# A diffusion transformer layer on one Trainium2 core: written order in the opening and both FFN1 down-projections, spilled chunks in rows of 4 KB, two conditioning vectors computed later

## The chip, the core and the metric

The kernel runs on one core of a Trainium2 chip. The core has a matrix engine (TensorE, called PE in the profile; its weight loads are PEld), three engines for elementwise work (VectorE or DVE, ScalarE or ACT, GpSimd or POOL), a queue that issues DMAs (SyncE or SP) and 16 DMA engines between on-chip memory (SBUF) and device memory (DRAM). Results of TensorE land in PSUM, eight banks of 2 KB a partition.

The metric is device microseconds for one launch of the whole layer. A launch can be profiled; the profile gives each instruction's start and duration, counted from the start of the span, and the clock that TensorE was granted as a share of full speed.

## The reference

One layer over 512 latent tokens (x) and 256 context tokens (ctx), model width 1024, all in float32:

```
ml, mc = adaln(c), adaln(c_ctx)          # silu(cond) @ w_mod + b_mod, 9 vectors of 1024 each
h  = x   + 0.5*ml[2]*rms(swiglu(rms(x)  *(1+ml[1])+ml[0]))*g      # FFN1, latent
hc = ctx + 0.5*mc[2]*rms(swiglu(rms(ctx)*(1+mc[1])+mc[0]))*g      # FFN1, context, same weights
k_c, v_c = keys, values of rms(hc)*(1+mc[4])+mc[3]
y  = mixer(rms(h)*(1+ml[4])+ml[3], k_c, v_c)   # differential attention and gated convolution, merged
h  = h + ml[5]*rms(y)*g
h  = h + 0.5*ml[8]*rms(swiglu(rms(h)*(1+ml[7])+ml[6]))*g          # FFN2, latent
swiglu(z) = (silu(z @ w_gate) * (z @ w_up)) @ w_down              # inner width 2816
```

The nine vectors are numbered m = 0 to 8 below. The context needs m = 0 to 4 only. The change touches FFN1, the vectors and the first part of the mixer (values and context keys).

## The kernel before

**Numbers.** A float32 operand is split into a high part that TensorE reads at its fast float32 format (`hi`, L62, a cast on ACT) and a low part, the rest (`lo`, L67, a subtraction on DVE, or on POOL for every n-th weight, n being `pool_share`). A product is three matmuls: high by high, high by low, low by high. So each weight of 128 x 1024 costs one DMA, one cast and one subtraction (`unit`, `split`) before TensorE can use it.

**Opening (0 to 88 us).** x and ctx lie side by side in 768 columns per group of 128 channels. ACT squares them and TensorE sums for the norm. The vectors 0 and 1 come in four steps, `mod_mm(i)` (matmuls) and `mod_col(i)` (transposing matmuls, then additions on DVE), each for two of the eight channel groups d. `mod_x(d)` scales and shifts group d and makes its high and low parts. `mod_t(p)` takes groups 2p and 2p+1: POOL makes four sums and differences of their column halves (tiles sqt, two buffers), and ACT and DVE make the high and low parts of these. In between, TensorE does the first two of 22 chunks of the inner width directly, in eight steps over k (`open_steps`, L144). `w_load`, `w_pool`, `w_dve`, `w_hi`, `w_lo` load the gate and up weights of a chunk and make sums, differences and their parts. What comes first on an engine in the opening is chosen by the scheduler, apart from a few `issue_after` marks on TensorE.

**Gate-up loop (88 to 395 us).** Chunks 2 to 21 use seven products of half size instead of eight (tiles A, K, G in PSUM banks pa, pb, pc). The first product of chunk 2 writes a pa buffer that the opening's chunks leave when ACT has taken silu of it (L606). Each finished chunk of 768 columns is spilled: high and low parts (tiles hh, hl) are stored with one DMA each. The loop stands inside `with self.in_order()`, which ties each instruction of PE, DVE, ACT and POOL to the one written before it on the same engine; SP is not tied. Vectors 2 and 3 are computed on the side (`mod_early`): `mod_acc` multiplies and adds rows of w_mod on DVE (L556, tiles macc, one 512 KB load for every two rows); `mod_sum` casts the result, sums over partitions on TensorE (tile pd, L107), copies a row on ACT (L572), writes it to DRAM (row_dram, L574), reads it back as columns (L579) and adds the bias on DVE (L581). These are generators; `take(mods, n)` runs n of their steps at fixed places, 5 a chunk.

**Down-projections (395 to 634 us).** `down` runs the 22 chunks twice, first for the 512 latent columns (eight PSUM banks b0 to b7), then for the 256 context columns. For each chunk it loads the spilled parts and one 128 x 1024 weight (f1d), splits the weight, and does 24 matmuls (L731). Beside the latent one, `mod_late` accumulates vectors 4 to 8, five steps a chunk. Beside the context one run the latent result's norm, gate, residual and next modulation (`sandwich`, the tiles yl, sqacc, sqt; taken as `chain`), and the `mod_sum` of vectors 4 to 8, three steps a chunk. Order is chosen by the scheduler here.

**Values and context keys (634 to 734 us).** `values(q, ts)` and `kv_ctx_k(j)` project both streams, while the context's `sandwich` runs as `chain`. Attention, merge and FFN2 follow.

Of the kernel before, what the change touches and what calls it, by code (L numbers as in the profile page):

```python
# [16 lines left out]
P = 128  # L17
# [22 lines left out]
class Builder:  # L40
# [137 lines left out]
    def build(self):  # L178
# [56 lines left out]
        hf_dram = self.t(dp, [NF, 2, P, NKEY], "hf_dram", F32R)  # L235
# [37 lines left out]
        t12, t34 = {}, {}  # L273
# [73 lines left out]
        lat3 = lambda t: t.rearrange("p (s n) -> p s n", s=3)[:, 0:3:2, :]  # L347

        def mod_x(d):

            x = xt[d]
            xl = lat3(x)
            nc.vector.scalar_tensor_tensor(out=xl, in0=xl, scalar=s1[:, 0, d:d + 1], in1=lat3(pbs),
                                           op0=ALU.mult, op1=ALU.mult)
            nc.scalar.activation(xl, xl, AF.Identity, bias=mst[:, 0, 0, d:d + 1], scale=1.0)
            xc = x[:, NCX:2 * NCX]
            nc.gpsimd.tensor_tensor(out=xc, in0=xc, in1=pbs[:, NCX:2 * NCX], op=ALU.mult)
# [6 lines left out]
            else:  # L364
                xeb[d] = self.t(hp, [P, 2, HK], ("hh", "hl")[d // 2 % 2], F32R, bufs=2)
# [5 lines left out]
        def mod_t(p):  # L371
# [9 lines left out]
            tt(out=v[:, 1, :], in0=x2[:, a], in1=u[:, 1, :], op=ALU.subtract)  # L381
            t12[p] = [slot(2 * p + hl, [P, 2, HK], F32R) for hl in range(2)]
# [106 lines left out]
        with tc.issue_after(spread):  # L489
            rows = {0: mod_mm(0)}  # L490
        with tc.issue_after(last["pe"]):
            mod_col(0, rows.pop(0))
        gu0 = [self.split(raw, DM, ring()) for raw in raws[:2]]
        with tc.issue_after(last["pe"]):
            rows[1] = mod_mm(1)
        mod_x(0)
        mod_x(1)
        gu1 = [self.split(raw, DM, ring()) for raw in raws[2:]]
        first = open_steps([gu0, gu1])
        next(first)  # L500
        for i in range(4):
            with tc.issue_after(last["pe"]):
                last["pe"] = next(first)
            if i < 3:
                with tc.issue_after(last["pe"]):
                    mod_col(i + 1, rows.pop(i + 1))
                mod_x(2 * i + 2)
                mod_x(2 * i + 3)
            mod_t(i)
            with tc.issue_after(last["pe"]):  # L510
                last["pe"] = next(first)
            if i < 2:
                with tc.issue_after(last["pe"]):
                    rows[i + 2] = mod_mm(i + 2)
            if i == 2:
                w_load(2)
                w_pool(2)
                w_dve(2)
                w_hi(2, 0)
                w_lo(2, 0)  # L520
                w_hi(2, 2)
                w_lo(2, 2)
# [841 lines left out]
```

## Time and profile before

| | us |
|---|---|
| median of 3 runs (lowest, highest) | 1685.35 (1683.03, 1690.57) |
| the profiled execution | 1684.36 |
| its span | 1682.5 |
| opening | 0 to 88.0 |
| gate-up loop | 88.0 to 395.0 |
| latent down-projection | 395.0 to 534.2 |
| context down-projection | 534.2 to 633.9 |
| values and context keys | 633.9 to 733.6 |
| the rest | 733.6 to 1682.5 |

The mean granted clock of TensorE is 0.984. The times of the stages are starts of the stage's first matmul or the end of the last one before it, from the span's start.

In the lists below a row reads: start, duration, engine, line and operation, output tile from input tiles, shape, count, and in square brackets the idle time before it with what ended it. In a row of waits: who waited for whom, us in total, times, longest. In a row of a group: line, engine, operation, count, then busy us, mean ns of one, and idle time before them.

### The profile page before, as it was taken

To read this page: it belongs to the slowest core of one execution; us is meant where nothing else is said; L and a number is where in the kernel's file an instruction comes from. 1 tells how busy PE (TensorE), PEld (TensorE's weight loads), DVE (VectorE), ACT (ScalarE), POOL (GpSimd) and SP (SyncE) were. 2 spreads that over 40 slices of the span, in tenths; PEclk is the share of its full clock that TensorE was granted. 3 is DMA by queue.
4 is the path that set the end of the run, shared out by engine and by line. 5 is a ranking of instruction groups with operands and counts; after the bars stand their busy time and mean duration, and the time that the engine had idled before them with its cause. 6 is when DMAs were issued, how large, how long until landed. Compare 5 with 4: busy or idle time off the path is not lost. (4 is left out here: it accounts for less than half of the span.)

```text
span 1682.5 us, 23537 instructions
## 1 busy us (share of the span) xinstructions
PE 1598.6 (95%) x8962; PEld 1418.3 (84%) x8962; DVE 1066.9 (63%) x1464; ACT 724.6 (43%) x1137; POOL 268.3 (16%) x205
## 2 busy tenths in 40 slices
PE   5999999998988899999999999999999999999996
PEld 4899999997866789988888888788889998888886
DVE  5687979785657757358877777473347843343345
ACT  4554444442113554335655556442237732222234
POOL 3434434430001232110000000000002100000003
PEclk9999999999999899999999999999999999999998
DMA  9144444447898775687565453632245743232321
GB/s 373 42 154 148 157 144 145 150 144 240 294 311 279 231 238 185 196 256 215 152 171 150 138 150 98 245 134 94 95 150 190 260 132 120 81 107 91 98 76 50
DMA packets 135769, 281.16 MB, mean 167 GB/s; under 512 B 23253, under 2 KB 67925, under 8 KB 135657
## 3 DMA queue, kind: packets, MB, share of 16 engines
q1 hardware_dynamic: 135656, 279.66, 51.7%
q8 instruction: 70, 1.15, 0.3%
q14 instruction: 43, 0.34, 0.1%
HBM read 228.72 MB, written 38.31 MB: 159 GB/s over the span
## 5 line engine op out<-in xcount | busy, mean ns | idle before, releaser
L62 ACT CAST whi<-wraw 128x1024 fp32r<-128x1024 f32 (+1 forms) x262 | 269.4, 1030 | 505.5 <-PE pa L107 95.2
L67 DVE TENSOR_TENSOR wlo<-wraw,whi 128x1024 fp32r<-128x1024 f32 (+1 forms) x250 | 329.4, 1319 | 201.9 <-ACT whi L62 194.5
L107 PE MATMUL f<-xs,whi 128*128 128x512 f32 x640 | 201.6, 394 | 0.0
L107 PE MATMUL pa<-xs,whi 128*128 128x512 f32 (+1 forms) x704 | 195.8, 362 | 0.7 <-ACT ob L968 0.5
L107 PEld LDWEIGHTS pa<-xs,whi 128*128 128x128 f32 x704 | 126.1, 189 | 21.0 <-ACT ob L968 0.7
L107 PEld LDWEIGHTS f<-xs,whi 128*128 128x128 f32 x640 | 118.3, 188 | 23.0
L731 PE MATMUL b<-hh,whi 128*128 128x512 f32 (+1 forms) x352 | 119.9, 352 | 11.5 <-ACT whi L62 7.9
L107 PE MATMUL pa<-xs,wlo 128*128 128x512 f32 (+1 forms) x352 | 127.1, 361 | 1.5 <-DVE wlo L67 1.5
L107 PE MATMUL f<-xs,wlo 128*128 128x512 f32 x320 | 125.1, 391 | 0.0
L731 PE MATMUL b<-hh,wlo 128*128 128x512 f32 (+1 forms) x352 | 112.2, 348 | 11.7 <-DVE wlo L67 6.8
L731 PE MATMUL b<-hl,whi 128*128 128x512 f32 (+1 forms) x352 | 118.4, 343 | 0.6 <-DMA hl<-hf_dram 0.6
L107 PE MATMUL pb<-xs,whi 128*128 128x512 f32 (+1 forms) x448 | 114.4, 344 | 0.0
L160 POOL TENSOR_TENSOR sqacc<-sqacc,sqt 128x256 f32<-128x256 f32 (+1 forms) x20 | 20.0, 1000 | 497.6 <-ACT sqt L158 496.2
L731 PEld LDWEIGHTS b<-hh,whi 128*128 128x128 f32 x352 | 69.7, 199 | 23.9 <-ACT whi L62 13.0
L107 PEld LDWEIGHTS pb<-xs,whi 128*128 128x128 f32 x448 | 78.1, 190 | 9.9
L731 PEld LDWEIGHTS b<-hh,wlo 128*128 128x128 f32 x352 | 65.4, 198 | 22.7 <-DVE wlo L67 10.4
L556 DVE SCALAR_TENSOR_TENSOR macc<-mraw,sc,macc 128x512 f32<-128x512 f32 x84 | 79.8, 1002 | 1.6 <-DMA mraw<-wmodr 1.6
L107 PE MATMUL pb<-xs,wlo 128*128 128x512 f32 (+1 forms) x224 | 77.2, 345 | 0.0
L107 PEld LDWEIGHTS pa<-xs,wlo 128*128 128x128 f32 x352 | 66.5, 189 | 11.7 <-DVE wlo L67 1.7
L731 PEld LDWEIGHTS b<-hl,whi 128*128 128x128 f32 x352 | 69.1, 196 | 8.2 <-DMA hl<-hf_dram 1.3
L936 ACT ACTIVATE e<-s,mx 128x768 f32<-128x768 f32 x64 | 57.1, 898 | 35.1 <-DVE mx L932 35.0
L107 PEld LDWEIGHTS f<-xs,wlo 128*128 128x128 f32 x320 | 60.1, 188 | 12.6
(371 smaller groups left out, 3685.2 us busy)
## 6 DMA issues: line engine op xcount, KB each, us to landing
mraw<-wmodr SPq DMA_DIRECT2D x56, 512.0 KB
wraw<-f2gu SPq DMA_DIRECT2D x56, 512.0 KB
wraw<-f1gu SPq DMA_DIRECT2D x44, 512.0 KB
wraw<-f1d SPq DMA_DIRECT2D x44, 512.0 KB
wraw<-f2d SPq DMA_DIRECT2D x24, 384.0 KB
hf_dram<-hh SPq DMA_DIRECT2D x22, 384.0 KB
hf_dram<-hl SPq DMA_DIRECT2D x22, 384.0 KB
wm<-wmod SPq DMA_DIRECT2D x16, 512.0 KB
```

The lines of the kernel that those rows point to most:

```text
L62: self.nc.scalar.copy(out=out, in_=src)
L67: (eng or self.nc.vector).tensor_tensor(out=out, in0=src, in1=hi.bitcast(F32), op=ALU.subtract)
L107: self.nc.tensor.matmul(out, lhsT=lhsT, rhs=rhs, start=start, stop=stop)
L160: eng.tensor_tensor(out=a, in0=a, in1=s, op=ALU.add)
L556: nc.vector.scalar_tensor_tensor(out=acc, in0=raw[:, k], scalar=s, in1=acc, op0=ALU.mult, op1=ALU.add)
L731: nc.tensor.matmul(o, lhsT=w[:, c], rhs=h[hl], start=start and f + j == 0, stop=f == NF - 1 and j == 2, skip_group_check=True)
L936: nc.scalar.activation(e[m], ps[:, m * NKEY:(m + 1) * NKEY], AF.Exp, scale=SCALE, bias=mx[:, 2 + m:3 + m], accum_out=mx[:, 4 + m:5 + m])
```

## The change

- The opening, and all from the first chunk of the latent down-projection to the end of the context one's chain, also stand under `in_order` (the latter by an ExitStack, closed after `drain(chain)`). The marks of `issue_after` there go.
- In the opening the 768 columns are laid out as half the context, the latent, half the context, and `mod_x` follows. `mod_t(p)` keeps POOL's sums; their parts are made by the new `mod_tp(p)`, one step later. `w_dve(2)` comes after two of the parts.
- A spilled chunk's parts are one tile h. The latent columns go to hl_dram, in rows of 512 x 2 x 4 bytes = 4 KB a partition, and the context's to hc_dram, rows of 2 KB: three DMAs for two. A load of the down-projection is one DMA instead of two.
- `down` loads and splits two chunks ahead (`fetch(f + 2)`). Its first spilled operand is loaded before the last chunk is spilled.
- `mod_sum` takes `wait` steps between its casts and its matmuls (4 in the loop, 3 in the context down-projection, 2 later) instead of one. `mod_late` beside the latent down-projection has vectors 4, 5 and 8, four steps a chunk; vectors 6 and 7 are accumulated and summed beside the values and keys. `pool_share` in the context one is 3 instead of 4.

```
-        hf_dram = self.t(dp, [NF, 2, P, NKEY], "hf_dram", F32R)
+        hl_dram = self.t(dp, [NF, P, 2, NT], "hl_dram", F32R)
+        hc_dram = self.t(dp, [NF, P, 2, NCX], "hc_dram", F32R)
...
+            tsum[p] = u, v
+
+        def mod_tp(p):
+            u, v = tsum.pop(p)
             t12[p] = [slot(2 * p + hl, [P, 2, HK], F32R) for hl in range(2)]
...
+        with self.in_order():
             rows = {0: mod_mm(0)}
...
+            for i in range(4):
+                next(first)
+                if i < 3:
                     mod_col(i + 1, rows.pop(i + 1))
+                    mod_x(2 * i + 2)
+                    mod_x(2 * i + 3)
+                if i:
+                    mod_tp(i - 1)
+                mod_t(i)
+                next(first)
...
+            mod_tp(3)
...
+            h = self.t(hp, [P, 2, NKEY], "h", F32R, bufs=2)
+            self.hi(h[:, 0], g)
+            self.lo(h[:, 1], g, h[:, 0])
+            self.move(hl_dram[f], h[:, :, P:P + NT])
+            for e in range(2):
+                self.move(hc_dram[f][:, :, e * P:e * P + P], h[:, :, e * 640:e * 640 + P])
...
-            yield
+            for _ in range(wait):
+                yield
...
+            h0 = self.t(hp, [P, 2, NT], "h", F32R, bufs=2)
+            self.move(h0, hl_dram[0])
             tail[2]()
             drain(mods)
...
+            fetch(0)
+            fetch(1)
             for f in range(NF):
+                if f + 2 < NF:
+                    fetch(f + 2)
...
-            take(mods, 5)
+        mods = mod_late(((4, (0, 1), 4), (5, (0,), None), (8, (0,), None)))
+        inorder.enter_context(self.in_order())
+        for _ in down(hl_dram, NT, [(p, True) for p in pl], {0: h0}, 0):
+            take(mods, 4)
...
+        for f, _ in enumerate(down(hc_dram, NCX, [(p, d % 2 == 0) for d, p in enumerate(pcs)], {}, 3)):
+            if f:
+                take(chain, 1)
             for _ in range(3):
                 next(next(sums, iter(())), None)
...
+        inorder.close()
...
+        mods = late_sums()
+        values(3, [0, 1, 2, 3, 4, 5])
+        take(mods, 12)
```

First place: POOL in the second half of the opening, before (xs are groups of x, sqt the sums of `mod_t`, s and wraw the weights of chunks 2 and 3).

```order
L357 TENSOR_TENSOR xs_50_145<-xs_50_145,pbs_248 128x256
...
L381 TENSOR_TENSOR sqt_531<-xs_46_137,sqt_530 128x384
L439 TENSOR_TENSOR s_142_715<-wraw_713 128x512
L440 TENSOR_TENSOR wraw_713<-wraw_711,wraw_713 128x512
L439 TENSOR_TENSOR s_172_872<-wraw_870 128x512
L440 TENSOR_TENSOR wraw_870<-wraw_868,wraw_870 128x512
L378 TENSOR_TENSOR sqt_661<-xs_47_139 128x384
...
L381 TENSOR_TENSOR sqt_662<-xs_48_141,sqt_661 128x384
L378 TENSOR_TENSOR sqt_765<-xs_49_143 128x384
```

The same place in the change:

```order
L384 TENSOR_TENSOR sqt_531<-xs_47_138,xs_46_136 128x384
L358 TENSOR_TENSOR xs_50_144<-xs_50_144,pbs_249 128x2x128
L358 TENSOR_TENSOR xs_51_146<-xs_51_146,pbs_249 128x2x128
L381 TENSOR_TENSOR sqt_660<-xs_48_140 128x384
...
L384 TENSOR_TENSOR sqt_661<-xs_49_142,sqt_660 128x384
L446 TENSOR_TENSOR s_137_706<-wraw_704 128x512
L447 TENSOR_TENSOR wraw_704<-wraw_702,wraw_704 128x512
L446 TENSOR_TENSOR s_169_871<-wraw_869 128x512
L447 TENSOR_TENSOR wraw_869<-wraw_867,wraw_869 128x512
L381 TENSOR_TENSOR sqt_764<-xs_50_144 128x384
```

The weight sums of chunks 2 and 3 stood ahead of mod_t(2) and mod_t(3); now mod_t(2) stands ahead of both, behind the last two groups of x, and mod_t(3) behind both.

Second place: DVE from the last chunk's spill (the low part from u) to the first accumulation of `mod_late`, before.

```order
L684 TENSOR_TENSOR u_3627<-n_623_3554,pb_3538 128x384
L581 TENSOR_TENSOR mcx_86<-mcx_86,vec_66 128x8
L67 TENSOR_TENSOR hl_3676<-u_3627,hh_3675 128x768
L553 TENSOR_SCALAR macc_3760<-mraw_3762,sc_80 128x512
L553 TENSOR_SCALAR macc_3761<-mraw_3762,sc_80 128x512
```

The same place in the change:

```order
L67 TENSOR_TENSOR h_3644<-u_3595,h_3644 128x768
L560 SCALAR_TENSOR_TENSOR macc_3524<-mraw_3650,sc_80,macc_3524 128x512
...
L560 SCALAR_TENSOR_TENSOR macc_3525<-mraw_3656,sc_80,macc_3525 128x512
L67 TENSOR_TENSOR mraw_3662<-macc_3524,mraw_3662 128x512
L586 TENSOR_TENSOR ml_85<-ml_85,vec_66 128x8
L67 TENSOR_TENSOR mraw_3672<-macc_3525,mraw_3672 128x512
L586 TENSOR_TENSOR mcx_86<-mcx_86,vec_66 128x8
L557 TENSOR_SCALAR macc_3773<-mraw_3775,sc_80 128x512
```

Eight accumulations of vector 3 (two shown), its two low parts and the two bias additions (L586, which read what came back from DRAM) moved behind the last spill. On PE the two sums of these parts, tiles pd, stand between the last product of the loop and the first matmul of the down-projection.

Third place: DVE in the context down-projection of the change (yl and sqacc are the latent chain; wlo the weights' low parts).

```order
L1265 TENSOR_TENSOR yl_623_3704<-yl_623_3704,res_4675 128x512
L586 TENSOR_TENSOR mcx_86<-mcx_86,vec_66 128x8
L225 SCALAR_TENSOR_TENSOR smc_88<-mcx_86,vec_66 128x8
L67 TENSOR_TENSOR mraw_5027<-xc_701_4081,mraw_5027 128x512
L1262 SCALAR_TENSOR_TENSOR yl_624_3705<-yl_624_3705,gp_14_90,b_812_4761 128x512
L160 TENSOR_TENSOR sqacc_0_817_4774<-sqacc_0_817_4774,sqt_5064 128x512
L67 TENSOR_TENSOR wlo_5078<-wraw_5075,whi_5077 128x1024
```

These rows run in this order now; the bias addition stands ahead of the low part of the weight. Before, nothing fixed them to the order of the program's text.

More of the change, by code (lines that the diff above doesn't have):

```diff
@@ L272, in build @@
         xeb = {}
-        t12, t34 = {}, {}
+        t12, t34, tsum = {}, {}, {}
         def load_mod(d):
@@ L729, in down @@
                     o, start = outs[d]
-                    for j, (w, hl) in enumerate(((wh, 0), (wh, 1), (wl, 0))):
-                        nc.tensor.matmul(o, lhsT=w[:, c], rhs=h[hl], start=start and f + j == 0,
+                    for j, (wt, hl) in enumerate(((wh, 0), (wh, 1), (wl, 0))):
+                        nc.tensor.matmul(o, lhsT=wt[:, c], rhs=x[:, hl], start=start and f + j == 0,
                                          stop=f == NF - 1 and j == 2, skip_group_check=True)
```

127 lines of the change are left out of this document (54 added, 73 removed).

## The prediction

> **What bounds the kernel now.** I read the windows by stage first, then the idle time of TensorE in each stage, then the list of each other engine around those places. The columns are the stretch, its length, then for PE, PEld, DVE, ACT and POOL the busy time with the count, then granted clock, DMA share and GB/s.
>
> ```profile
> PE 1598.6 (95%) x8962; PEld 1418.3 (84%) x8962; DVE 1066.9 (63%) x1464; ACT 724.6 (43%) x1137; POOL 268.3 (16%) x205
> ...
> 21.10:88.00 66.90, 58.22 (x449) 51.99 (x449) 43.55 (x63) 34.16 (x52) 33.35 (x28) 0.90 0.40 152
> 88.00:395.00 307.00, 300.73 (x1697) 295.15 (x1696) 257.54 (x280) 141.06 (x220) 114.77 (x75) 0.99 0.44 151
> 395.00:534.20 139.20, 126.09 (x528) 98.49 (x528) 87.91 (x118) 24.30 (x28) 0.99 (x1) 0.99 0.90 302
> 534.20:633.90 99.70, 83.89 (x585) 78.13 (x586) 70.78 (x91) 52.18 (x78) 33.19 (x17) 0.91 0.74 231
> 633.90:733.60 99.70, 96.20 (x786) 95.52 (x785) 50.57 (x82) 41.44 (x69) 20.73 (x14) 0.98 0.63 203
> ...
> 420.00:440.00 20.00, 20.00 (x90) 16.57 (x89) 16.41 (x23) 3.16 (x3) 0.00 (x0) 1.00 0.88 304
> 500.00:520.00 20.00, 18.24 (x78) 13.99 (x76) 12.17 (x15) 3.19 (x4) 0.00 (x0) 1.00 0.92 322
> ```
>
> TensorE bounds nearly all of it (95%), so a gain can only come out of its gaps. The five stages are the opening, the gate-up loop, the latent and the context down-projection, and the values with the context keys; from 733.6 on nothing is touched. The stretch 420 to 440 shows TensorE never idle: 20.00/90 = 0.222 us a matmul of 512 columns, so 24 of them, one chunk, take 5.33 us, and 22 chunks 117.3. The latent stage has 139.2, some 22 above that. A context matmul has half the columns, so by the same rate 22 chunks take 58.7 and the stage, with 57 other matmuls, has at least 30 us in which TensorE is not at its pace. So both down-projections have something to win; what the written order gives back of it is the question.
>
> **Opening: +11 us, from -6 to +13.** TensorE loses its time here to two short stalls and the half clock behind them.
>
> ```profile
> 63.47 0.44 PE L144 MATMUL pa<-xe,whi 128*128 128x384 f32 x1 [3.20 <-ACT xe L62]
> ...
> 64.60:71.30 6.70, 5.96 (x24) 5.96 (x25) 4.20 (x4) 2.16 (x3) 3.23 (x3) 0.50 0.01 4
> ```
>
> The stall before step k=4 costs 3.2, and the 6.7 us at a granted clock of 0.50 behind it cost half of that, 3.4. In the new order the third column of modulation vectors stands on DVE ahead of the sums' low parts, so I let this stall go: TensorE would end the eight steps some 6 earlier than 88.0. That is the lower end, -6.
>
> But POOL's order changes too (the first excerpt). mod_t(2) now waits for the low parts of mod_tp(1), since the two sum buffers are shared, and these stand on DVE behind x6 and x7.
>
> ```profile
> 58.43 1.28 POOL L439 TENSOR_TENSOR s<-wraw 128x512 f32<-128x512 f32 x1 [4.97 <-DVE wlx L67]
> 62.43 0.99 POOL L378 TENSOR_TENSOR sqt<-xs 128x384 f32<-128x384 f32 x1 [1.38 <-ACT xs L355]
> 75.83 1.02 POOL L378 TENSOR_TENSOR sqt<-xs 128x384 f32<-128x384 f32 x1 [8.01 <-ACT xs L355]
> 79.48 1.72 POOL L381 TENSOR_TENSOR sqt<-xs,sqt 128x384 f32<-128x384 f32 x1
> ...
> 56.04 0.69 DVE L446 TENSOR_TENSOR s<-wraw,s 128x512 f32<-128x512 f32 x1
> 56.04 1.05 ACT L62 CAST whx<-s 128x1024 fp32r<-128x1024 f32 x1 [3.96 <-DVE s L445]
> 57.12 1.23 DVE L67 TENSOR_TENSOR wlx<-s,whx 128x1024 fp32r<-128x1024 f32 x1 [0.39 <-ACT whx L62]
> 81.23 0.84 ACT L62 CAST wm<-sqt 128x768 fp32r<-128x768 f32 x1 [0.84 <-POOL sqt L381]
> 82.09 1.28 ACT L606 ACT_TABLE_LOAD   x1
> 84.37 0.60 ACT L606 ACTIVATE g<-pa 128x512 f32<-128x512 f32 x1 [1.00 <-PE pa L144]
> ```
>
> One mod_t takes 75.83 to 81.20, 5.4. Before, mod_t(2) ran at 62.43 and only mod_t(3) waited, to 75.83, for x6. Now mod_t(2) itself stands behind x6 and x7, and I give it that start, 75.8: its vectors come about 6 earlier, and the low parts of x6, x7 and mod_tp(1) that are put in front of it on DVE take about that. Then, each behind the other: mod_t(2) to 81.2; the weight sum of chunk 2, 1.28, to 82.5; DVE's difference, 0.69, to 83.2; ACT's high part, 1.05, to 84.2; DVE's low part, 1.23, to 85.5. POOL's two sums for chunk 3 wait for this low part, as the row at 58.43 shows (s<-wraw, released by DVE wlx): 2.6, to 88.1. Behind them comes mod_t(3), 5.4, to 93.5, then ACT's last high part 0.84, the table load 1.28 and the first silu 0.6, which stand behind it on ACT: 96.2. That silu frees the PSUM buffer pa that the first product of chunk 2 writes. So TensorE stands from 82 to 96.2, where in the profiled run it went on at 88.0: +8.2. If the half clock behind so long a gap is that behind the gap of 3.2, it adds up to 3.4: +11, with 2.8 of these. The upper end adds 2 for a mod_t(2) that starts so much later.
>
> **Gate-up loop: -5 us, from -7 to -3.** Each modulation sum now waits 4 steps between its casts and its matmuls on TensorE, where it waited one:
>
> ```profile
> PE pd L107 <- ACT mraw L62: 2.8, 3, 1.1
> PE pd L107 <- DVE mraw L67: 2.5, 6, 0.5
> ```
>
> Both waits, 5.3 together, are for those casts, and with three steps more between they go, but for those at the end of the loop. The third DMA of each chunk's spill is hidden by the stage's DMA share of 0.44; SP, which issues it, is named in neither wait.
>
> **Boundary and latent down-projection: +3 us, from -7 to +8.** The early sums took 100 steps, 20 chunks of 5. With three more steps for each of 8 sums they take 124, so 24 are left to the end of the loop, and the order puts them ahead of the down-projection (the second excerpt).
>
> ```profile
> 394.61 0.34 PE L624 MATMUL pa<-xo,wlx 128*128 128x384 f32 x1
> 397.99 0.95 DVE L67 TENSOR_TENSOR hl<-u,hh 128x768 fp32r<-128x768 f32 x1
> 398.55 0.85 PE L731 MATMUL b<-hh,whi 128*128 128x512 f32 x2 [3.60 <-DMA hh<-hf_dram]
> ...
> L556 DVE SCALAR_TENSOR_TENSOR macc<-mraw,sc,macc 128x512 f32<-128x512 f32 x28 | 19.1, 744 | 1.6 <-DMA mraw<-wmodr 1.6
> 385.38 0.69 DVE L67 TENSOR_TENSOR mraw<-macc,mraw 128x512 fp32r<-128x512 f32 x1
> 377.81 0.38 SPq L579 DMA_DIRECT2D ml<-row_dram  x1
> 380.07 0.17 DVE L581 TENSOR_TENSOR ml<-ml,vec 128x8 f32<-128x8 f32 x1 [0.83 <-DMA ml<-row_dram]
> 390.54 0.24 SPq L574 DMA_DIRECT2D row_dram<-macc  x1
> 393.41 0.39 SPq L579 DMA_DIRECT2D mcx<-row_dram  x1
> 397.90 0.17 DVE L581 TENSOR_TENSOR mcx<-mcx,vec 128x8 f32<-128x8 f32 x1 [4.45 <-DMA mcx<-row_dram]
> ```
>
> The spill's low part can end at 398.4 (in the profiled run DVE stood before it, at the addition that waited for a read-back). Then 8 accumulations of 0.744, to 404.3; the low part of the first sum, 0.69, to 405.0; two matmuls, ACT's copy, together some 1.2, to 406.2; the row written and the write landed, 390.54 to 393.41, 2.9; the read-back, 2.3 (377.81 to 380.07) to 4.5 (393.41 to 397.90): 411.4 to 413.6. DVE waits for it before the second sum's low part (0.7), and TensorE does that sum's matmuls (0.6) before the down-projection. It starts near 413, where it started at 398.55.
>
> Behind it, the accumulations took 5 steps a chunk and take 4, and two of the five vectors leave. So the heaviest chunks of the old stage loaded 2.5 blocks of 512 KB of modulation weights beside the chunk's own weights and its spilled operand, 2.36 MB; now chunks 0 to 7 load 1.57 MB, 8 to 15 2.10 MB and the rest 1.05 MB. At 322/0.92 = 350 GB/s (500 to 520, where TensorE is idle for 1.8 of 20 us) 2.10 MB take 6.0 us against 5.33: 5.3 us over eight chunks, of which the prefetch of two chunks and the light chunks ahead hide some. I take 3.5. Then 413 + 117.3 + 3.4 (half clock behind the gap) + 3.5 = 537.2, against 534.2: +3. The ends: no slip and a start at 406.2, with the read-back hidden, -7; a start at 414.6 and all of 7 lost, +8.
>
> The opening's loads have pieces of 3 to 4 KB, and their rate stands in the window
>
> ```profile
> 20.00:40.00 20.00, 15.30 (x117) 11.56 (x117) 12.31 (x16) 10.51 (x16) 12.82 (x12) 0.83 1.02 406
> ```
>
> at 406/1.02 = 398 GB/s a full share. By it the eight chunks take 5.27 us each and the slip is nothing. The rule of the Trainium skill ("DMA: Bandwidth & Descriptors", section "Specifications") is that a transfer of 512 bytes already moves at line rate; by it the 4 KB rows in place of 1 KB rows win nothing and the slip is the 5.3 above. The trace, 398 against 350, speaks against it by 14%, though other queues differ too in these windows. By the one the sum would be 3.5 lower, by the other 2 higher.
>
> **Context down-projection: +3 us, from -15 to +10.** What ACT, DVE and POOL do in this stage, by form, with the idle time ahead of them:
>
> ```profile
> L67 POOL TENSOR_TENSOR wlo<-wraw,whi 128x1024 fp32r<-128x1024 f32 x12 | 30.6, 2549 | 96.0 <-ACT whi L62 95.9
> L67 DVE TENSOR_TENSOR wlo<-wraw,whi 128x1024 fp32r<-128x1024 f32 x18 | 23.9, 1329 | 14.6 <-ACT whi L62 14.6
> L1239 DVE SCALAR_TENSOR_TENSOR yl<-yl,gp,b 128x512 f32<-128x512 f32 x8 | 5.6, 740 | 1.2 <-PE b L107 1.2
> L1242 POOL TENSOR_TENSOR yl<-yl,res 128x512 f32<-128x512 f32 x4 | 5.5, 1384 | 18.4 <-DVE yl L1239 18.4
> L62 ACT CAST whi<-wraw 128x1024 fp32r<-128x1024 f32 x27 | 28.0, 1043 | 18.5 <-DMA wraw<-f1d 11.5 <-PE b L731 6.5 <-DMA wraw<-wv 0.4
> L158 ACT ACTIVATE sqt<-yl 128x512 f32<-128x512 f32 x12 | 7.4, 631 | 5.1 <-DVE yl L1242 1.8 <-POOL sqacc L160 1.3 <-POOL yl L1242 1.0
> ```
>
> ACT now does its evictions and squares of the latent result, ten and more of 0.5 to 0.63, before the first weight's high part, and a low part of 2.55 on POOL comes behind: with some weights made ahead, TensorE starts about 6 late. In the 8 chunks that carry the chain of the latent norm one step hangs on the other through the queues: high part 1.04, low part 1.33, gate 0.74, residual sum 1.38 on POOL (0.7 on DVE), square 0.63; 4.4 to 5.1, partly beside the next, against 2.67 of TensorE. I take 4.5, so 8 x 1.8 = 14. And DVE's additions of a read-back row (the third excerpt) stand in order before low parts of weights, while SP issues the read only behind a write: one stall of about 9 (2.9 for the write, 4.5 for the read, and a low part of 2.55 that SP waits for, less a step) and four of 1.5 to 4.5 (write and read less the three steps between), 20 in all. 58.7 + 6 + 14 + 20 and 4 of half clock are 103, against 99.7: +3. With 5 of the 20 it is -12, with a start 3 earlier -15; with 4.5 for each read +10. I take the middle, since DVE's list shows the additions ahead of the weights that they hold up.
>
> **Values and keys: +2 us, from -2 to +6.** Sixteen loads of 512 KB, 32 accumulations of 0.744 and four sums move in. DVE has 50.57 + 24 of 99.7, the DMA share goes from 0.63 by 8.4 MB at about 340 GB/s a quarter up, under 0.9. So these are hidden by TensorE's products, 96.20 of the 99.7; four sums on TensorE, about 0.6 each, are the 2. Cover gone costs a read-back, 4.5; a granted clock of 1.00 instead of 0.98 would win 2.
>
> The sum is 11 - 5 + 3 + 3 + 2 = +14 on the profiled execution's 1684.4 (span 1682.5 and 1.9 around it), which lies 1.0 below the median of 1685.35: 1698.4, I say 1698.
>
> **The rivals.** *A, faster, chance 0.17:* the context down-projection runs at TensorE's pace. For it: 11.5 of ACT's 18.5 us of idle time there waits for the loads of weights, which the prefetch of two chunks takes away, and two chunks' parts made ahead may lie beside the present chunk's products. Against it: DVE's order, which couples them. With 58.7 + 6 + 10 of read-backs and clock the stage takes 75, and 1698 - 28 = 1670. It decides where the parts of a chunk, overlapped with the next, take under 2.67 us.
> *B, about the same, 0.22:* POOL's chain in the opening is short, because mod_t(2) starts 6 earlier with its vectors. The first product then comes at 90, with some half clock +3 instead of +11, and the latent stage slips by nothing: 1698 - 8 - 3 = 1687.
> *C, slower still, 0.07:* the read-backs take 4.5 us each in every place: +10 for the context stage and +5 more at the boundary and in the latent stage, 1698 + 7 + 5 = 1710.
>
> **How the numbers follow.** My forecast, 0.54, has its own range of 1690 to 1708. The range of 8 in 10 reaches down towards A, 1675, and up to C, 1711. About 0.5%, 8.4 us, is what a measurement of this kernel can tell from no change, so the same is 1677 to 1694. Faster is A and a little of B's lower edge, 0.18; the rest of B and the lower edge of the forecast are the same, 0.27; what is left, 0.55, is slower.
>
> **What would show it.** In the changed profile: no wait for xe before k=4; mod_t(3) on POOL behind the weight sums, and a gap on TensorE of over 10 us before the first 384-column product, with granted clock 0.50 behind it; no waits of pd for mraw in the loop; eight accumulations and a read-back between 398 and 413; 24 matmuls at 5.3 to 5.5 us from there; in the context stage, DVE standing at L586 with <-DMA ml<-row_dram. The prediction is wrong if the first product starts before 90, if the first chunk of the latent stage starts before 406, or if the context stage takes under 85 us.

## The result, and the profile after

The changed kernel takes 1710.49 us (median of 4 runs, 1709.31 to 1712.62), the kernel before 1685.39 beside it: a ratio of 1.0146, 95% interval 1.0120 to 1.0172. It is slower by about 25 us. The time lies in the range that was given, near its upper end, and 12 us above the forecast of 1698.

The windows by stage, first of the kernel before, cut where one stage's last matmul ends, then of the changed one (the columns as in the prediction):

```profile
88.00:394.90 306.90, 300.68 (x1697) 295.15 (x1696) 257.54 (x280) 141.04 (x219) 114.77 (x75) 0.99 0.44 151
533.90:634.00 100.10, 84.03 (x587) 78.23 (x587) 71.18 (x91) 52.58 (x79) 33.19 (x17) 0.91 0.74 231
634.00:768.30 134.30, 130.58 (x939) 123.55 (x938) 73.12 (x117) 53.34 (x86) 25.89 (x18) 0.99 0.70 212
```

```profile
97.80:397.00 299.20, 298.00 (x1692) 294.97 (x1692) 245.82 (x269) 141.01 (x217) 111.91 (x75) 0.99 0.47 154
397.00:413.40 16.40, 2.86 (x4) 1.37 (x5) 8.95 (x14) 3.04 (x5) 1.51 (x2) 0.66 0.38 113
534.40:648.60 114.20, 82.05 (x579) 77.92 (x579) 58.12 (x71) 45.43 (x63) 34.49 (x18) 0.84 0.60 188
648.60:793.10 144.50, 133.94 (x947) 124.80 (x946) 106.88 (x165) 62.96 (x104) 31.87 (x21) 0.99 0.83 250
```

The last row of each reaches to attention's first transposing matmul (t<-ident,a). Set against the prediction's terms, in us:

| stage | before | after | predicted | measured |
|---|---|---|---|---|
| opening, to the first product of chunk 2 | 88.0 | 97.8 | +11 | +9.8 |
| gate-up loop | 306.9 | 299.2 | -5 | -7.7 |
| boundary and latent down-projection | 139.0 | 137.4 | +3 | -1.6 |
| context down-projection | 100.1 | 114.2 | +3 | +14.1 |
| values, keys, to attention | 134.3 | 144.5 | +2 | +10.2 |
| the rest of the span | 914.2 | 914.1 | 0 | -0.1 |
| sum | 1682.5 | 1707.2 | +14 | +24.7 |

What TensorE waited for in the changed kernel, stage by stage (us in total, times, longest):

```profile
PE pa L629 <- ACT g L611: 15.9, 1, 15.9
PE pa L629 <- ACT n L672: 0.6, 2, 0.3
PE pa L629 <- ACT n L651: 0.5, 1, 0.5
...
PE pd L107 <- ACT mraw L62: 10.5, 2, 9.3
PE b L744 <- ACT whi L62: 7.9, 1, 7.9
PE pd L107 <- DVE mraw L67: 3.1, 1, 3.1
...
PE b L107 <- ACT mraw L62: 12.8, 3, 10.8
PE b L107 <- DVE mraw L67: 4.9, 4, 3.7
PE b L107 <- DVE rstd_d L138: 4.4, 2, 4.3
```

The first row is the gap at the opening's end, the next two are all that is left in the loop (the waits of 2.8 and 2.5 for mraw are gone). The three rows after them lie at the two ends of the latent stage, the last three in the context stage. In between TensorE is full: from 420 to 520 it is never idle.

(In the first row of the excerpt of POOL's order in the change, the inputs of the sum at L384 are xs_47_138 and sqt_530; nothing rests on it.)

### The profile page after: what moved, and what is told of

It reads as the page before. It is cut to its first block, busy times and chain, and to the rows that moved or that the text cites. A ratio compares the mean times of both kernels' runs of the same rounds, so it can differ in the third digit from the quotient of the medians.

```text
span 1707.2 us, 23531 instructions
## 1 busy us (share of the span) xinstructions
PE 1593.7 (93%) x8962; PEld 1420.3 (83%) x8962; DVE 1057.7 (62%) x1463; ACT 727.9 (43%) x1139; POOL 272.6 (16%) x208
## 5 line engine op out<-in xcount | busy, mean ns | idle before, releaser
L744 PE MATMUL b<-h,whi 128*128 128x512 f32 (+1 forms) x704 | 178.5, 345 | 7.9 <-ACT whi L62 7.9
L744 PEld LDWEIGHTS b<-h,whi 128*128 128x128 f32 x704 | 127.0, 199 | 23.0 <-ACT whi L62 8.3
L744 PE MATMUL b<-h,wlo 128*128 128x512 f32 (+1 forms) x352 | 121.2, 344 | 2.1 <-POOL wlo L67 2.1
L560 DVE SCALAR_TENSOR_TENSOR macc<-mraw,sc,macc 128x512 f32<-128x512 f32 x112 | 101.0, 940 | 3.7 <-DMA mraw<-wmodr 3.3
L744 PEld LDWEIGHTS b<-h,wlo 128*128 128x128 f32 x352 | 69.5, 198 | 9.5 <-POOL wlo L67 2.6
L872 POOL TENSOR_TENSOR rot<-rot,cossin 128x512 f32<-128x512 f32 x16 | 22.6, 1411 | 252.7 <-DVE rot L871 231.5
L1166 DVE TENSOR_TENSOR silu<-silu,pb 128x512 f32<-128x512 f32 (+1 forms) x28 | 16.0, 573 | 67.0 <-PE pb L107 66.5
```

The source lines that it names most:

```text
L560: nc.vector.scalar_tensor_tensor(out=acc, in0=raw[:, k], scalar=s, in1=acc, op0=ALU.mult, op1=ALU.add)
L744: nc.tensor.matmul(o, lhsT=wt[:, c], rhs=x[:, hl], start=start and f + j == 0, stop=f == NF - 1 and j == 2, skip_group_check=True)
L872: nc.gpsimd.tensor_tensor(out=rt, in0=rt, in1=cs[:, 1, :], op=ALU.mult)
L1166: nc.vector.tensor_tensor(out=a[:, :n], in0=a[:, :n], in1=pu[:, :n], op=ALU.mult)
```

## The experiments

Each is the changed kernel with one edit, until the last four, which join edits. Each ratio is to the kernel before on the same chip. That kernel's median was 1685.0, 1686.9 and 1682.4 in the three groups, so gains are compared by ratios: 0.1% is 1.7 us.

**1. The opening: parts of the sums made earlier.**

```
                 next(first)
+                if i:
+                    mod_tp(i - 1)
                 if i < 3:
                     mod_col(i + 1, rows.pop(i + 1))
                     mod_x(2 * i + 2)
                     mod_x(2 * i + 3)
-                if i:
-                    mod_tp(i - 1)
                 mod_t(i)
```

> The changed kernel, but the parts of the sums (mod_tp(i - 1)) are made before the next column and the next two groups of x, not behind them. Theory: the opening's loss comes from POOL, which waits for the two shared sum buffers; freed earlier, mod_t(2) starts near 61 us and not at 76.9, the weight sums of chunk 3 near 83 and not 87, the first product of chunk 2 near 91 and not 97.8, so the whole takes 6 to 9 us less than the changed kernel's 1710.5: about 1703. Rival: mod_t(3) stands behind the weight sums of chunk 3 on POOL, and these wait for DVE's low part whatever mod_t(2) does; then the first product stays within 2 us of 97.8 and the time within 2 us of 1710.5.

Measured: 1704.95, ratio 1.0120 (1.0095 to 1.0144). POOL's list, of the changed kernel and then of this one:

```profile
76.85 1.66 POOL L381 TENSOR_TENSOR sqt<-xs 128x384 f32<-128x384 f32 x1 [6.97 <-DVE xs L67]
...
87.22 1.91 POOL L446 TENSOR_TENSOR s<-wraw 128x512 f32<-128x512 f32 x1 [1.76 <-DVE wlx L67]
91.03 0.99 POOL L381 TENSOR_TENSOR sqt<-xs 128x384 f32<-128x384 f32 x1
```

```profile
67.28 1.66 POOL L381 TENSOR_TENSOR sqt<-xs 128x384 f32<-128x384 f32 x1 [7.40 <-DVE xs L67]
...
83.63 1.92 POOL L446 TENSOR_TENSOR s<-wraw 128x512 f32<-128x512 f32 x1 [8.42 <-DVE wlx L67]
87.45 0.99 POOL L381 TENSOR_TENSOR sqt<-xs 128x384 f32<-128x384 f32 x1
```

mod_t(2) starts 9.6 earlier, but POOL then stands 8.4 for wlx, and mod_t(3) comes 3.6 earlier only; so does the first product, 94.2. Theory and rival each hold a part: the shared buffers cost something, the weight sums ahead of mod_t(3) more.

**2. All of the early sums in the loop.**

```
-                take(mods, 2)
+                take(mods, 3)
...
-                take(mods, 3)
+                take(mods, 4)
```

> The changed kernel with 7 steps of the early sums a chunk of the gate-up loop (3 and 4) instead of 5 (2 and 3), so that the 124 steps end inside the loop. Theory: the 24 steps left over are what TensorE waits for between the loop and the latent down-projection (16.5 us, 397.0 to 413.4); without them the down-projection starts some 6 us behind the last product, and the time falls by 10 to 12 us, with the half clock behind the gap: about 1699. Rival: DVE is busy for 246 of 299 us in the loop, and the steps push its products' parts back, so the loop grows by as much (8 accumulations of 0.74 us and two sums, 6 to 8 us) and the time falls by less than 4 us.

Measured: 1712.93, ratio 1.0167 (1.0142 to 1.0192): no gain. The gap of 16.4 before the down-projection is gone, but for a wait of 5.6 for a spilled operand, and the loop takes 311 us in place of 299. The rival had the sign. In the loop TensorE now waits 9.2 for the copy n of L672, where it waited 0.6:

```profile
PE pa L629 <- ACT n L672: 9.2, 7, 3.8
```

The longest of these waits, in the lists of ACT and PE:

```profile
140.59 0.62 ACT L62 CAST mraw<-macc 128x512 fp32r<-128x512 f32 x1 [2.73 <-DVE macc L560]
141.11 1.04 ACT L62 CAST whx<-s 128x1024 fp32r<-128x1024 f32 x1
142.06 0.47 ACT L672 COPY n<-pa 128x384 f32<-128x384 f32 x1
```

```profile
142.58 0.62 PE L629 MATMUL pa<-xs,whi 128*128 128x384 f32 x2 [3.81 <-ACT n L672]
```

ACT's cast of a finished sum waits for DVE's last accumulation, and behind it in the written order stands the copy that frees pa. At this place it is not DVE's sum of work but where in the chunk a sum ends; the other six waits, 5.4 together, were not followed.

**3. More steps between a read-back and its use.**

```
             yield
+            if wait == 3:
+                yield
+                yield
+                yield
...
-                     for x in [mod_sum(fp, psf, "b4", 1, m, q, v, 3)] * 7])
+                     for x in [mod_sum(fp, psf, "b4", 1, m, q, v, 3)] * (6 + 4 * q)])
```

> The changed kernel, but in the context down-projection three more steps (one chunk) lie between the read-back of a row and DVE's addition of the bias. Theory: DVE stands at the addition (7.8 us at 577.6 to 585.4) with the low parts of weights behind it in the order, and TensorE with it (10.8, 3.7 and 4.3 us before the sums); with a chunk between, these waits fall to under 2 us each, the stage shrinks from 114 us by 10 to 18 and the time is about 1697. Rival: the stage is set by ACT's and DVE's work of the latent chain in a fixed order, and the wait only shows there; then it shrinks by less than 4 us.

Measured: 1700.4, ratio 1.0098 (1.0070 to 1.0125). The wait in question, in the changed kernel's lists of DVE and of SP:

```profile
585.42 0.17 DVE L586 TENSOR_TENSOR ml<-ml,vec 128x8 f32<-128x8 f32 x1 [7.79 <-DMA ml<-row_dram]
```

```profile
577.48 0.24 SPq L579 DMA_DIRECT2D row_dram<-macc  x1
...
581.18 0.39 SPq L584 DMA_DIRECT2D ml<-row_dram  x1
```

The read is issued 3.7 after the write, and the addition runs 4.2 later; DVE stands until then, with the latent chain and the low parts behind it. With a chunk between, the context stage takes 101.4 us and not 114.2, and TensorE's longest wait for a sum's parts there is 4.9, not 10.8. The 7.9 at the stage's start stays:

```profile
PE b L107 <- ACT mraw L62: 9.7, 3, 4.9
PE b L748 <- ACT whi L62: 7.9, 1, 7.9
```

The theory holds for 13 us of the stage, though not to "under 2 us each"; 2 of them are lost again in the values (146.7 against 144.5).

**4. Pieces of 1 KB again.**

```
-            self.move(hl_dram[f], h[:, :, P:P + NT])
             for e in range(2):
+                self.move(hl_dram[f, e], h[:, :, P + e * 256:P + e * 256 + 256])
...
-                    self.move(h[f], src[f])
+                    if n == NCX:
+                        self.move(h[f], src[f])
+                    else:
+                        for e in range(2):
+                            self.move(h[f][:, :, e * 256:e * 256 + 256], src[f, e])
```

> The changed kernel with the latent columns of the spill in two pieces of 256 columns, so that loads and stores move pieces of 1 KB, as before the change (two loads a chunk instead of one). Theory: the rows of 4 KB are why TensorE lost nothing in the latent down-projection (384 GB/s at a DMA share of 1.00 from 500 to 520 us); with 1 KB the share there reaches 1 at about 345 GB/s, 2.1 MB a chunk take 6.1 us against 5.4, and the stage grows by 3 to 6 us: about 1715. Rival, by the rule of the Trainium skill (DMA: Bandwidth & Descriptors, Specifications) that 512 bytes already move at line rate: nothing changes, and the stage's gain is all from fewer loads a chunk and the prefetch; the time stays within 1.5 us of 1710.5.

Measured: 1709.66, ratio 1.0150 (1.0126 to 1.0173): no change. The heaviest window of the latent stage, with 4 KB and then with 1 KB:

```profile
500.00:520.00 20.00, 20.00 (x90) 16.53 (x90) 9.36 (x10) 4.21 (x4) 0.00 (x0) 1.00 1.00 384
```

```profile
500.00:520.00 20.00, 20.00 (x90) 16.56 (x89) 8.64 (x9) 4.21 (x4) 0.00 (x0) 1.00 0.99 353
```

TensorE is full in both. A full share carries 384 GB/s in the first and 353/0.99 = 357 in the second. But run 1, with rows of 4 KB too, has 345/0.97 = 356 in this window:

```profile
500.00:520.00 20.00, 20.00 (x90) 16.57 (x89) 6.28 (x7) 4.21 (x4) 0.00 (x0) 1.00 0.97 345
```

From 420 to 520 it is 325/0.93 = 349 with 1 KB, and 353 to 360 in run 1, run 3 and the changed kernel: 1 to 3% apart. The rival holds. The rule of the Trainium skill ("DMA: Bandwidth & Descriptors", section "Specifications") that stands with it agrees with the time, and no difference in rate shows here that is clear of the spread between runs.

**5. Without vectors 6 and 7.** The accumulations and sums of these two beside the values are left out, and both are set to zero.

```
-        mods = late_sums()
+        mods = iter(())
+        nc.vector.memset(ml[:, 48:64], 0.0)
+        make_scale(s2l, ml, 7, V_PRE2)
```

> The changed kernel without the work on vectors 6 and 7 beside the values: 16 loads, 32 accumulations, four sums are left out and the two vectors are set to zero, so the output is not the reference's. Theory: DVE is at 86 of 109 us there with that work and TensorE is short of parts from 653 to 693; without it the stretch from the first value product to the first attention product (144.5 us, 134.3 before the change) shrinks by 6 to 9 us, and the time to about 1703. Rival: the loss there comes from the end of the latent chain, of which five modulations are left when the context down-projection ends; the vectors lie beside TensorE's products, and the stretch shrinks by less than 3 us (the four sums on TensorE).

Measured: 1705.17, ratio 1.0107 (1.0089 to 1.0126), 0.38% less than the changed kernel's. In the trace the stretch is 2.4 shorter:

```profile
648.70:790.80 142.10, 132.88 (x939) 124.72 (x938) 78.48 (x129) 59.72 (x96) 30.16 (x21) 0.98 0.69 207
```

DVE has 28 us less to do, and TensorE is hardly fuller (93.5% of the stretch against 92.7%). The four sums that are left out are 2.5 us of TensorE in the changed kernel, which is the whole difference, and most of the waits there stay: 3.2 for sqacc, 1.7 for yc and 1.4 for xs, where the changed kernel has 3.4, 1.9 and 3.6. In the stage the rival holds (under 3). The time fell by more, 0.38% or some 6 us, of which the profiled execution shows 3.9; the rest stays open.

**6. Two steps of the latent chain a chunk.**

```
-                take(chain, 1)
+                take(chain, 1 if f < 12 else 2)
```

> The changed kernel, taking two steps of the latent chain a chunk from chunk 12 of the context down-projection on, as before the change, instead of one throughout. Theory: the modulations left over to the values (five of eight) then run inside the down-projection; the values no longer wait for the latent operand (1.3, 1.9 and 1.4 us), and the stretch from values to attention falls by 3 to 6 us, while the context stage grows by 0 to 4, its last ten chunks having about 3 us of TensorE each for twice the chain: about 1708. Rival: in a fixed order two modulations a chunk (of some 2.2 us of DVE each, with a low part of 1.2) pass TensorE's 2.9 us, the context stage grows by over 6, and nothing is won.

Measured: 1717.86, ratio 1.0180 (1.0151 to 1.0209), 0.34% above the changed kernel's, with intervals that overlap. The two stages:

```profile
535.00:657.30 122.30, 84.35 (x577) 79.62 (x578) 65.48 (x82) 50.80 (x72) 34.52 (x20) 0.82 0.57 178
657.30:800.30 143.00, 133.89 (x947) 126.13 (x946) 95.85 (x154) 57.27 (x95) 29.79 (x19) 0.98 0.81 250
```

The down-projection grows by 8.1, the values shrink by 1.5: the rival. TensorE's waits for xs and yc in the values are gone, but waits of 4.7 for sqacc and 2.7 for rstd_d stand in their place, so pulling the chain's tail in does not give back what the values lost.

**7. No written order in the context down-projection.**

```
             self.sqadd(fp, sqyl, yl[d], d, NT)
+        inorder.close()
...
         drain(chain)
-        inorder.close()
```

> The changed kernel with the written order closed behind the latent down-projection, so that the scheduler sets the context down-projection's order again, the chunks still fetched two ahead. Theory: what the context stage lost (114 us against 99.7 from the last latent matmul on) is the fixed order, which puts DVE's additions of a read-back row ahead of parts of weights; without it the stage takes 96 to 103 us, and the whole about 1699. Rival: the stage is long by its fewer steps of chain and its third of the low parts on POOL (2.5 us each) whatever the order; then it stays within 4 us of 114.

Measured: 1670.13, ratio 0.9902 (0.9882 to 0.9922), 2.4% under the changed kernel and faster than the one before. The stage, and what TensorE and DVE waited for in it (all of TensorE's, and the last of DVE's):

```profile
535.00:608.60 73.60, 71.27 (x579) 69.94 (x578) 57.90 (x73) 46.01 (x65) 34.70 (x18) 1.00 0.77 248
```

```profile
PE b L107 <- DVE sqacc L160: 1.4, 1, 1.4
PE b L744 <- POOL wlo L67: 1.0, 1, 1.0
```

```profile
DVE ml L586 <- DMA ml<-row_dram: 0.5, 1, 0.5
```

The instructions are the same, and the stage takes 73.6 us and not 114.2: TensorE is busy for 71.3 of it, at full clock (0.84 in the written order). DVE's whole wait for read-backs is 0.5. The theory holds, and its price of 11 to 18 us was far too low: the fixed order cost 40.

**8. Another written order in the opening.** The parts of a sum follow it at once, the last group's sums are on DVE, and the parts of chunk 2's third operand come behind the first silu.

```
                 next(first)
+                if i in (1, 2):
+                    mod_tp(i - 1)
                 if i < 3:
...
-                if i:
-                    mod_tp(i - 1)
-                mod_t(i)
+                    mod_t(i)
...
                     w_hi(2, 0)
+                    mod_tp(2)
+                    mod_t(3, nc.vector)
+                    mod_tp(3)
                     w_lo(2, 0)
                     w_dve(2)
-                    w_hi(2, 2)
-                    w_lo(2, 2)
-            mod_tp(3)
...
             plain_tail(0, ps0[0])
+            w_hi(2, 2)
+            w_lo(2, 2)
```

> The changed kernel with another written order in the opening: the parts of the first three sums come as soon as these are there, the last group's sums are made on DVE (0.55 us each) behind the parts of the third, and two parts of chunk 2's weights come behind the first silu. POOL's weight sums of chunk 3 then hold nothing up. Theory: the first product of chunk 2 starts near 88 us and not 97.8, the gap before it is some 4 us and not 15.9, and the time falls by 9 to 12 us: about 1700. Rival: the opening is bound by ACT's and DVE's parts and not by POOL, so that the first product stays above 93 us and the time falls by no more than the first experiment's 5.5.

Measured: 1699.21, ratio 1.0075 (1.0057 to 1.0093).

```profile
84.18 0.61 PE L629 MATMUL pa<-xe,whx 128*128 128x384 f32 x2 [1.99 <-ACT g L611]
89.54 0.62 PE L629 MATMUL pb<-wm,whi 128*128 128x384 f32 x2 [3.00 <-ACT whi L62]
```

The first product starts at 84.2, 13.6 earlier, behind a gap of 2.0 in place of 15.9. A gap of 3.0 before the second product gives some of it back. The theory holds, and more than holds for the start (88 was expected): ACT and DVE had the time for this work. That POOL's queue held the opening fits it; but the run also moves two parts behind the first silu, and the two were not separated.

**9 to 12. Joined.** Run 9 has the edits of 7 and 8. Run 10 adds a move of vector 3's second half out of the loop:

```
-            for m in (2, 3):
-                for q in range(2):
+            for m, qs in ((2, (0, 1)), (3, (0,))):
+                for q in qs:
...
-        mods = mod_late(((4, (0, 1), 4), (5, (0,), None), (8, (0,), None)))
+        mods = mod_late(((3, (0, 1), None), (4, (0, 1), 4), (5, (0,), None), (8, (0,), None)))
...
```

Run 11 is run 10 without the prefetch, run 12 is run 10 with the values in their old order:

```
-            fetch(0)
-            fetch(1)
             for f in range(NF):
-                if f + 2 < NF:
-                    fetch(f + 2)
+                fetch(f)
```

```
-        for q in range(3):
+        for q in range(2):
             values(q, [2, 3, 4, 5])
-            take(chain, 8)
+            take(chain, 10)
...
-        values(3, [0, 1, 2, 3, 4, 5])
-        take(mods, 12)
-        for q in range(3):
+        for q in range(2, 4):
+            values(q, [0, 1, 2, 3, 4, 5])
+            take(mods, 8)
+        for q in range(2):
             values(q, [0, 1])
             take(mods, 8)
```

> The changed kernel with both mends at once: no written order in the context down-projection, and the other written order in the opening. Theory: the two losses lie in stages that do not touch each other, so the gains add: 1710.5 - 40.4 - 11.3 = 1659, within 3 us. Rival: part of the opening's gain is given back in the gate-up loop, or what the context stage wins is waited for in the values; then over 1664.

> The kernel of the run before it, with the second half of vector 3 (its 16 accumulations and two sums) moved out of the gate-up loop, to the latent down-projection and the context one. 92 steps are left for the loop's 100, so none stands between the loop and the down-projection, and none is pressed into the loop. Theory: TensorE's 16.5 us between the last product of the loop and the first latent matmul shrink to about 4 to 6, and the time falls by 9 to 12 us, to about 1648. Rival: as with seven steps a chunk, the work is paid where it goes: eight loads of 512 KB more and 12 us of DVE in the latent down-projection, two sums more in the context one; then the time falls by less than 5 us.

> The kernel of the run before it, but each chunk of both down-projections is loaded and split where its matmuls stand, not two chunks ahead. Theory: the prefetch in the program's text is what gave the context stage 73.6 us in free order against 99.7 before the change: there ACT waited 81 us for loads of weights, queued on SP behind a row's write; without it the stage goes back to 85 to 100 us and the time rises by 10 to 25 us. Rival: the gain comes from the four sums fewer and the spilled chunk in one load; the text's order of loads matters little to a scheduler that is free, and the time rises by less than 4 us.

> The kernel of the second run of this group, with the values in the order of before (two passes over the latent tokens alone, two over all, two over the context's) in place of three, one and three, the two late vectors beside them. Theory: a seventh pass costs two more weights to load and split (about 1.2 us of DVE and 1 of ACT each) and a later drain of the context's chain; leaving out the vectors or the chain's tail each gave back 1.5 to 2.5 of the 10 us, so the rest should be this order: the time falls by 4 to 7 us, to about 1642. Rival: three passes over the latent tokens are needed to cover the context's chain, and with two TensorE waits longer for it; the time rises or stays within 2 us.

| run | median us | ratio to before (95%) |
|---|---|---|
| 9 | 1664.12 | 0.9887 (0.9864 to 0.9910) |
| 10 | 1663.79 | 0.9888 (0.9865 to 0.9911) |
| 11 | 1660.12 | 0.9863 (0.9837 to 0.9890) |
| 12 | 1654.55 | 0.9840 (0.9814 to 0.9866) |

Run 9: the gains do not add fully; by the ratios 0.15% of the 0.71% that the opening gave alone are left, 2.5 us of 12, and by the medians 6. At the start of the down-projection it is 10.8 ahead of run 7, in the span 5.6: each later stage gives one or two back. That is the rival, with no one place to name.

Run 10: the gap before the down-projection is gone, and its first matmul comes 14.9 earlier than in run 9, with the loop at 303.6 against 302.2, not grown as in experiment 2. The time is the same. Six come back at once, as a wait for the spilled operand and the half clock behind it, and 8.4 in the stretch from values to attention, 155.6 us in place of 147.2. The first, in the waits of TensorE and in the list of SP:

```profile
PE b L746 <- DMA h<-hl_dram: 5.8, 1, 5.8
```

```profile
392.41 1.54 SPq L72 DMA_DIRECT2D hc_dram<-h  x2
394.05 1.05 SPq L72 DMA_DIRECT2D h<-hl_dram  x2
```

The operand of chunk 0 was read in time, and TensorE does its matmuls from 388.2 to 393.8. It waits for that of chunk 1, which SP asks for only behind the stores of the last spill. In the kernel's text this operand takes one of the two buffers h that the spill uses, so it was to be expected. The 8.4 in the values were not.

Run 11: the time does not rise without the prefetch, the rival. In its profiled execution, 6 us above its median, the context stage is 82.0, 5.4 longer than in run 10; by this one execution the prefetch is a fifth of the fall from 100.1 to 73.6 in experiment 7. (The 81 us of waiting for weights that the theory names are ACT's in both down-projections; in the context one they were 11.5.) What the rest of that fall is from (four sums fewer, one load a chunk for two, other steps) was not taken apart.

Run 12: 0.48% less than run 10, 8 to 9 us, and 1.6% under the kernel before: the fastest of all. The stretch from values to attention is 146.8, against 155.6 in run 10. It is still 12.5 above the kernel before.

## Why the prediction was right where it was, and wrong where it wasn't

**Opening, right in mechanism and size.** Row for row: mod_t(2) started at 76.9 (75.8 in the walk), chunk 3's weight sums at 87.2 (85.5), the first silu at 97.2 (95.6), the first product at 97.8 (96.2). The stall before k=4 did go. Experiment 8 shows that the order was the cause: a new one gave back 13.6 of the start. The half clock behind the gap, priced at 2.8 here, cost 1.9 (0.52 for 4 us) and lies in the loop in the table above; counted with the opening, the two stages are +11.7 and -9.6.

**Gate-up, right, larger.** The sums' waits went, 5.3 as priced. The rest was not priced: the old loop's last whole chunk took 18.7 us, with 1.6 of these waits and a granted clock of 0.57 from 368 to 372 behind them, 1.7 lost; the longest of the new one after the first takes 15.3. That leaves 2 to 3 us open.

**Boundary, right to the microsecond; the latent stage behind it, wrong by the slip.** The start was put at 413 and came at 413.4, by some luck. The accumulations ended 2 later than in the walk (406.2 for 404.3), and the row's write and read-back took 3.6, from 408.4 to 412.0, where the walk had 5.2 to 7.4:

```profile
408.43 0.25 SPq L579 DMA_DIRECT2D row_dram<-macc  x1
412.03 0.17 DVE L586 TENSOR_TENSOR ml<-ml,vec 128x8 f32<-128x8 f32 x1 [5.08 <-DMA ml<-row_dram]
413.45 1.05 PE L744 MATMUL b<-h,whi 128*128 128x512 f32 x2
```

The 3.5 for the DMA were nothing: no chunk but the first was held up, and the stage, put at +3, came to -1.6. Against it, 5.33 a chunk was 5.44 (21 chunks start from 420.0 to 528.8), 2.4 over the stage. Experiment 4 shows that the rows' length is no part of it, and run 11 that the prefetch is none: without it the last 20 chunks start 5.44 apart too, from 407.1 to 510.5. That the lighter chunks (2.10 MB for 2.36) are the cause, and not one load a chunk for two, is argued only. Runs 10 and 12 carry four loads more there (28 for 24, and not the eight of the expectation), and their chunks from the third on also take 5.4.

**Context stage, the failed step: the size of the sum, term by term.** It was put at 103 and took 114.2. The mechanism (DVE's additions in order ahead of the weights, SP's read behind a write) is the one that the trace shows. The terms: the pace, 58.7, was 22 x 2.87 = 63.1, by the quickest chunks (the rate of 512 columns halved was too fast); the start, 6, was 7.9; the read-backs with their half clock, 24, were 26.7, in three chunks of 15.9, 9.1 and 10.3; what is left for the chain's coupling, 14, is 16.5. All four were too small, 11.5 together. Rival A was the truth of a kernel that wasn't this one: without the order the stage takes 73.6, against A's 75.

**Values and keys, the step that failed outright.** "Most is hidden" was put at +2 and cost 10.2. TensorE's waits there sum to 10.5 in the changed kernel and to 3.6 before (its largest rows, from 649 to 793 and from 633.9 to 768.4):

```profile
PE b L107 <- DVE sqacc L160: 3.4, 1, 3.4
PE b L820 <- POOL xs L67: 2.2, 2, 1.3
PE b L820 <- DVE yc L775: 1.9, 1, 1.9
PE b L820 <- DVE xs L170: 1.4, 1, 1.4
```

```profile
PE b L107 <- DVE sqacc L160: 2.2, 1, 2.2
```

The waits for xs are the end of the latent chain, 3.6, those for sqacc and yc the start of the context's. So 7 of the 10.2 are waits for chains that come late, which no term of mine had; I had counted the work moved in, not the chain left over. The four sums moved in are 2.5, as put, and in experiment 5 most of the waits stand without any of that work. What would give it back stays open: leaving out the late vectors gave 2.4 in the stretch, the chain's tail 1.5, and the old order of the passes 8.8 on top of run 10, which itself had lost 8.4 there. All three at once were not tried.

**The chances.** Slower had 0.55. The forecast's own range, 1690 to 1708, was missed by 2.5. The total is nearer than its terms: the first three stages came to 8.5 less than forecast and the last two to 19.3 more, and that these partly cancel is luck. C, at 1710, named the number but not the place, since the boundary and the latent stage were no worse than forecast.

## What to carry to other kernels

Fixing an order makes every wait of an instruction a wait of all that stands behind it on its engine. So before fixing one, look in each engine's list for the instructions that wait for a round trip (a DMA write and read-back, another engine's queue), and put a whole period of work between the issue and the use, or leave that stage to the scheduler: here the same instructions took 114.2 us in written order, 101.4 with a chunk between, and 73.6 in free order.

Where work is moved to a later stage, price what that stage then waits for as well as what it holds: the stretch of the values was 8 to 21 us longer than before in every kernel here, and its added work alone does not explain that (7.8 without it, in experiment 5).

## What the runs showed of the hardware

A gap of TensorE can be paid twice, in idle time and in clock, and its length alone does not say whether. In run 8 a gap of 2.0 us at 82.2 is followed by full clock (1.00 to 86.5), one of 3.0 at 86.5 by half:

```profile
91.00:93.00 2.00, 2.00 (x6) 2.00 (x7) 1.10 (x3) 1.10 (x2) 1.92 (x2) 0.50 1.04 250
```

In a part that no run changes, TensorE waits 1.8 us for the last sum of squares (pc<-ones,sqacc). Behind this wait the clock was half in the kernel before, and full in run 2:

```profile
1286.50:1289.50 3.00, 3.00 (x15) 3.00 (x15) 2.71 (x6) 0.26 (x1) 0.00 (x0) 0.50 1.02 349
```

```profile
1315.50:1318.50 3.00, 3.00 (x27) 3.00 (x27) 3.00 (x8) 1.46 (x3) 0.00 (x0) 1.00 0.95 309
```

The Trainium skill ("TensorE: Matmul & The Clock Gate", section "HAM oscillation — how this bites in real kernels") names idle gaps of more than about 3.4 us as what to avoid; here the shorter ones of 3.0 and 1.8 were enough, as was 3.2 in the opening of the kernel before. Nor does a longer gap cost more clock. Behind the 15.9 us of the changed kernel it was

```profile
98.00:102.00 4.00, 4.00 (x13) 4.00 (x14) 3.10 (x5) 2.60 (x5) 0.00 (x0) 0.52 0.00 1
...
103.00:105.00 2.00, 1.48 (x9) 1.16 (x8) 1.28 (x2) 2.00 (x4) 0.00 (x0) 1.00 1.13 264
```

at 0.52 for four microseconds and back at 1.00 five after the gap's end. Behind the 3.0 of run 8 it was still at 0.50 from 95 to 97, over five after that gap's end.
